# Attention probabilities of the last two query tiles turned by VectorE blocks and a trip through DRAM, with their value products put off

## The chip, the cores and the metric

The kernel runs on one core of a Trainium2 chip. The metric is the time of one execution on the device in microseconds (us). Five engines work side by side in that core: TensorE (PE in the rows; PEld is its loading of weights), VectorE (DVE), ScalarE (ACT), GpSimd (POOL) and SyncE (SP), which issues all of this kernel's transfers. The core has an on-chip memory of 128 partitions (SBUF) and the accumulation banks that TensorE writes (PSUM).

## The reference, cut to what matters

The model is a trunk of two layers over 1024 positions of width 1024. Each layer runs a convolution branch and a sparse attention branch from one input projection and joins them in one output projection. The change lies in the attention branch:

```python
def block_fn(args):                      # one block of 128 queries (blk = 0..7)
    ...
    score = jnp.einsum("bth,bths->bts", w_b, jax.nn.relu(s_raw))
    _, sel = lax.top_k(score, k_top)     # 256 keys for each query
    ...
    logits = logits + bias.astype(jnp.float32)
    probs = jax.nn.softmax(jnp.where(valid, logits, -jnp.inf), axis=-1)
    return jnp.einsum("bthk,btkc->bthc", probs.astype(kv.dtype), kv_sel)
...
y = jnp.concatenate([y_conv, y_attn], axis=-1) @ w_out[l]
```

There are 8 heads. The kernel doesn't gather: it computes the logits against all earlier keys and pushes the unselected ones out with a large constant, so query tile i (128 queries, i = 0 to 7) has 128 * (i + 1) keys.

## The kernel before, in words

**Order of a layer.** Projections, indexer and convolution run first, then `topk` picks keys, then `attention` (line 801), then `Split` (line 912) cuts the two branch outputs into a high and a low float32r part, then `out_proj` (line 933) multiplies them by the output weights in four column groups g = 0 to 3, and the next layer follows. Layer 0's attention lies at about 355 to 545 us of the profile, layer 1's at about 985 to 1147 us.

**Attention.** The heads are taken in pairs, pr = 0 to 3, and within a pair the query tiles in couples c: tiles 2c and 2c+1. The order of c is 0, 1, 2, 3 in the first three pairs and `LASTC` = 3, 1, 2, 0 in the last. For each couple, for each of the two heads e and the two tiles ii:
- `probs` (line 818) multiplies queries by keys into PSUM (tile `lg`, three float32r products a piece, lines 112 to 114), adds bias and mask (GpSimd line 837 or 834), takes the row minimum on VectorE (lines 843 and 847), the exponential on ScalarE (line 850), the reciprocal (line 851), and scales on GpSimd (line 852). The result `p` has queries on partitions.
- `transposed` (line 859) turns `p` by TensorE, 128x128 at a time (line 865), into PSUM (tag `tp`, two banks), and copies it to tiles `pt` in turn by ScalarE (line 870) and VectorE (line 872), so that keys lie on partitions.

Then the value products of the couple (line 893) run into one PSUM bank (`av`, tag `mm`), alternating between the two heads, and VectorE multiplies by the gate (line 896). Each of these matmuls stands as two records in the profile.

**Queries.** `queries(h)` (line 803) makes the high and low query tile of one head, in two halves of 512 columns through a PSUM bank of tag `mm` (`uq`), and loads the head's bias (`tb`). The next pair's two heads are called for after the second and the third couple of a pair.

**Buffers.** Every tag has a fixed number of buffers, and a tile whose tag has none free waits until one is released after its last reader. Those that matter: `hp`, 6 buffers of 4 KB a partition: four for the two heads in work (high and low each), two left; the high halves `yh` of `Split` use the same tag (four for the convolution branch `yc`, two for the attention branch `ya`, which shares its tile with `An` and stands so in the rows). `hq`, 6, for `pt`. `hv`, 4, for the values `v`, and later two of the `yh`. `t4`, 5, for `p`. PSUM `mm`, 2 banks, shared by `av`, `uq` and half of the output tiles `o`; `lg`, 4 banks. `pl`, 1, used by `topk` and then by the second half of the output weights of group 0.

**Who orders the work.** In attention no order is written out by hand: a list scheduler places each instruction on its engine's in-order queue, earlier lines of the program first where several are ready, at the times of its own timing model. `tc.issue_after(x)` only orders an instruction behind x on x's engine. All transfers go out by SyncE's in-order queue.

**Around the end of attention.** In the last pair, parts of `Split(yc)` are called for after each couple; `Split(ya)` follows attention. In `out_proj`, group 0 takes the query tiles in the order 6, 7, 2, 3, 4, 5, 0, 1, and each output tile sums eight k: 0 to 3 from `yc`, 4 to 7 from `ya`.

Of the kernel before, what the change touches and what calls it, by code (L numbers as in the profile page):

```python
# [11 lines left out]
F32 = mybir.dt.float32  # L12
# [11 lines left out]
P = 128  # L24
# [52 lines left out]
def hybrid_kernel(ctx: ExitStack, tc: tile.TileContext, x, cT, w_ada, w_mod, bcol, bgate, g_pre, w_in, w_cp,  # L77
# [20 lines left out]
    def st(tag, shape, dt=F32, name=None, bufs=None):  # L98
        return sb.tile(shape, dt, name=name or tag, tag=tag, bufs=bufs or BUFS.get(tag, 1))
# [701 lines left out]
    def attention(l, cq, kv, v, sc, sga, wq, select, yc):  # L801

        def queries(h):
            qt = [st("hp", [P, 1024], FR, name="q%d" % i) for i in range(2)]
            for half in range(2):
                hs = slice(512 * half, 512 * half + 512)
                o = mm_ps("uq")
                for k in range(2):
                    mm3(o, tuple(x_[:, 128 * h:128 * h + 128] for x_ in wq[k]),
                        (cq[:, k, hs], cq[:, 2 + k, hs]), k == 0, k == 1)  # L810
                S.activation(qt[0][:, hs], o, AF.Copy, scale=-QSCALE)
                V.scalar_tensor_tensor(qt[1][:, hs], o, -QSCALE, f32(qt[0][:, hs]), op0=OP.mult,
                                       op1=OP.subtract)
            tb = st("t5", [P, 256], name="tb")
            nc.sync.dma_start(tb, td[h])
            return qt, tb

        def probs(q, tb_, i):

            w = P * (i + 1)  # L820
            o = []
            for c0, c1 in pieces(i):
                o.append((lg_ps("lg"), c0, c1))
                mm3(o[-1][0][:, :c1 - c0], tuple(x_[:, 128 * i:128 * i + 128] for x_ in q),
                    tuple(x_[:, c0:c1] for x_ in kv), True, True)
            n0 = max(0, w - 256)
            nw = w - n0
            tb = tb_[:, 256 - nw:]
            p = st("t4", [P, 1024], name="p")
            nb = p[:, n0:w]  # L830
            if i < 2:
                if nw > 128:
                    V.tensor_copy(nb[:, 0:nw - 128], tb[:, 0:nw - 128])
                G.affine_select(nb[:, nw - 128:nw], tb[:, nw - 128:nw], pattern=[[-1, P]],
                                compare_op=OP.is_ge, fill=BIG, base=0, channel_multiplier=1)
            else:
                G.tensor_tensor(nb, tb, sc[:, OFF[i] + n0:OFF[i] + w], op=OP.add)  # L837
            m = st("mx", [P, 3], name="mx", bufs=8)
            lo = FMAX
            for o_, c0, c1 in o:  # L840
                if c0 < n0:
                    e = min(c1, n0)
                    V.tensor_tensor_reduce(out=p[:, c0:e], in0=o_[:, :e - c0], in1=sc[:, OFF[i] + c0:OFF[i] + e],
                                           scale=1.0, scalar=lo, op0=OP.add, op1=OP.min,
                                           accum_out=m[:, c0 // 384:c0 // 384 + 1])
                    lo = m[:, c0 // 384:c0 // 384 + 1]
            V.tensor_tensor_reduce(out=nb, in0=o_[:, n0 - c0:w - c0], in1=nb, scale=1.0, scalar=lo,  # L847
                                   op0=OP.add, op1=OP.min, accum_out=m[:, 2:3])
            ri = st("ri", [P, 2], name="ri", bufs=8)
            mark[0] = S.activation(p[:, :w], p[:, :w], AF.Exp, scale=-1.0, bias=m[:, 2:3], accum_out=ri[:, 0:1])  # L850
            V.reciprocal(ri[:, 1:2], ri[:, 0:1])  # L851
            mark[1] = G.tensor_scalar(p[:, :w], p[:, :w], ri[:, 1:2], 1.0, op0=OP.mult, op1=OP.mult)  # L852
            return p

        turn = [0]
        late = [[], []]
        mark = [None, None]

        def transposed(p, i, ii, pts):

            for j0 in range(0, i + 1, 4):
                n = min(4, i + 1 - j0)
                t = tp_ps("pt")
                for j in range(n):
                    T.transpose(t[:, 128 * j:128 * j + 128], p[:, 128 * (j0 + j):128 * (j0 + j) + 128], ident)  # L865
                dst = pts[j0 // 4][:, 0:n, 128 * ii:128 * ii + 128]
                src = t[:, :128 * n].rearrange("p (j t) -> p j t", j=n)
                turn[0] += 1
                if turn[0] % 2:
                    late[1].append(S.activation(dst, src, AF.Copy).ins)  # L870
                else:
                    late[0].append(V.tensor_copy(dst, src).ins)  # L872

        nxt = [queries(0), queries(1)]
        for pr in range(4):
            cur = nxt
            nxt = []
            if pr == 1:
                dump(f"sel{l}", sc)
            for at, c in enumerate((0, 1, 2, 3) if pr < 3 else LASTC):  # L880
                pts = [[st("hq", [P, 4, 256], name="pt") for _ in range(1 + c // 2)] for e in range(2)]
                for e in range(2):
                    for ii in range(2):
                        i = 2 * c + ii
                        p = probs(*cur[e], i)
                        transposed(p, i, ii, pts[e])
                o = mm_ps("av")
                for j in range(2 * c + 2):
                    for e in range(2):
                        h = 2 * pr + e  # L890
                        lh = v[j // 2][:, j % 2, 64 * h:64 * h + 64]
                        t0 = 128 if j == 2 * c + 1 else 0
                        T.matmul(o[64 * e:64 * e + 64, t0:256], lh, pts[e][j // 4][:, j % 4, t0:256],  # L893
                                 start=j == 0, stop=j == 2 * c + 1)
                g = sga[:, pr, 256 * c:256 * c + 256]
                V.tensor_tensor(g, o[:, :256], g, op=OP.mult)
                if (pr, c) == (2, 2):
                    with tc.issue_after(mark[0].ins), tc.issue_after(mark[1].ins):
                        w0 = wo_load(l, 0, 0)
                if at in (1, 2) and pr < 3:  # L900
                    nxt.append(queries(2 * pr + 2 + (at == 2)))
                if pr == 0 and at < 2:
                    select(4 + at)
                elif pr == 3 and at < 3:
                    with tc.issue_after(late[0][-1]), tc.issue_after(late[1][-1]):
                        if at == 0:
                            ys = Split(yc, ["hp"] * 4)
                        for n in range(3 * at, min(3 * at + 3, 8)):
                            ys.part(n // 2, 512 * (n % 2), 512, V)
        return w0, ys  # L910
# [332 lines left out]
```

## Time and profile before

| | us |
|---|---|
| median of 3 runs | 1235.65 (1235.15 to 1236.28) |
| the profiled execution, its own time | 1234.0 |
| the profiled execution, span of the trace | 1232.2 |
| TensorE busy in the span | 1173.8 (95%) |
| VectorE, ScalarE, GpSimd busy | 897.0, 701.9, 606.5 |

The time of an execution holds 1.8 us around its span. Busy shares are averages over stages that have different limits; what a change in one stage is worth is read from the rows of that stage.

### The profile page before, as it was taken

To read this page: it belongs to the slowest core of one execution; us is meant where nothing else is said; L and a number is where in the kernel's file an instruction comes from. 1 tells how busy PE (TensorE), PEld (TensorE's weight loads), DVE (VectorE), ACT (ScalarE), POOL (GpSimd) and SP (SyncE) were. 2 spreads that over 40 slices of the span, in tenths; PEclk is the share of its full clock that TensorE was granted. 3 is DMA by queue.
4 is the path that set the end of the run, shared out by engine and by line. 5 is a ranking of instruction groups with operands and counts; after the bars stand their busy time and mean duration, and the time that the engine had idled before them with its cause. 6 is when DMAs were issued, how large, how long until landed. Compare 5 with 4: busy or idle time off the path is not lost.

```text
span 1232.2 us, 23069 instructions
## 1 busy us (share of the span) xinstructions
PE 1173.8 (95%) x7832; PEld 975.8 (79%) x7832; DVE 897.0 (73%) x2182; ACT 701.9 (57%) x1616; POOL 606.5 (49%) x1218
## 2 busy tenths in 40 slices
PE   6999999999987999999999999999999599999998
PEld 3788888877875777789989888888798377777998
DVE  4657788898798656757686688898888876667214
ACT  4545767766864556643254376785687355566221
POOL 4431136547548548635483211553864665685222
PEclk9999999999998999999999999999999699999999
DMA  9520258852100001148651122894111000021205
GB/s 352 201 85 18 69 195 274 275 171 75 35 27 1 9 10 47 33 127 292 235 196 34 46 52 74 270 289 160 58 30 43 1 10 5 6 77 63 76 18 189
DMA packets 93158, 130.20 MB, mean 106 GB/s; under 512 B 41576, under 2 KB 70768, under 8 KB 93040
## 3 DMA queue, kind: packets, MB, share of 16 engines
q1 hardware_dynamic: 93040, 128.73, 32.5%
q8 instruction: 62, 1.02, 0.3%
q14 instruction: 56, 0.46, 0.1%
HBM read 115.06 MB, written 13.64 MB: 104 GB/s over the span
## 4 chain that ended last, share of the span: by engine, by line
PE 85%; DVE 5%; POOL 5%; issue 2%; ACT 1%; DMA 1%; SPq 0%; DVEq 0%; POOLq 0%; ACTq 0%
PE av L893 7%; PE pt L865 5%; PE ixs L476 5%; PE u L112 5%; PE u L113 5%; PE u L114 5%; PE g L112 5%; PE g L114 4%; PE g L113 4%; PE o L112 4%; PE o L113 4%; PE o L114 4%; PE lg L112 3%; PE cv L674 2%; PE lg L113 2%; PE lg L114 2%
## 5 line engine op out<-in xcount | busy, mean ns | idle before, releaser
L559 DVE TENSOR_SCALAR_CACHE_REDUCE jv<-pl,cand 128x768 int8<-128x768 uint16 (+1 forms) x186 | 187.9, 1010 | 30.8 <-POOL cand L566 20.0
L554 ACT ACTIVATE ja<-pl,cand 128x896 int8<-128x896 uint16 (+1 forms) x186 | 154.1, 829 | 60.6 <-POOL cand L566 45.7
L850 ACT ACTIVATE p<-p,mx 128x128 f32<-128x128 f32 (+7 forms) x128 | 98.7, 771 | 57.1 <-DVE mx L847 49.1
L852 POOL TENSOR_SCALAR p<-p,ri 128x128 f32<-128x128 f32 (+7 forms) x128 | 99.6, 784 | 39.6 <-DVE ri L851 39.2
L133 POOL TENSOR_TENSOR wul<-raw,wuh 128x342 fp32r<-128x342 f32 (+1 forms) x48 | 46.9, 1000 | 129.3 <-ACT wuh L132 123.3
L112 PE MATMUL o<-woh,yh 128*128 128x256 f32 x384 | 109.5, 286 | 0.0
L114 PE MATMUL o<-woh,yl 128*128 128x256 f32 x384 | 108.6, 283 | 0.0
L113 PE MATMUL o<-wol,yh 128*128 128x256 f32 x384 | 108.1, 282 | 0.0
L865 PE MATMUL pt<-ident,p 128*128 128x128 f32 x576 | 94.4, 282 | 10.2 <-POOL p L852 7.7
L112 PE MATMUL u<-hT,wuh 128*128 128x512 f32 x256 | 101.4, 396 | 0.0
L112 PE MATMUL g<-hT,wgh 128*128 128x512 f32 x256 | 101.2, 395 | 0.0
L114 PE MATMUL u<-hT,wul 128*128 128x512 f32 x256 | 100.0, 391 | 0.0
L113 PE MATMUL u<-hT,wuh 128*128 128x512 f32 x256 | 99.9, 390 | 0.0
L113 PE MATMUL g<-hT,wgh 128*128 128x512 f32 x256 | 99.8, 390 | 0.0
L114 PE MATMUL g<-hT,wgl 128*128 128x512 f32 x256 | 99.7, 389 | 0.0
L837 POOL TENSOR_TENSOR p<-tb,score 128x256 f32<-128x256 f32 x96 | 75.5, 793 | 47.4 <-PE pt L865 47.3
L893 PE MATMUL av<-pt,v 128*64 128x256 f32 (+1 forms) x640 | 94.9, 372 | 1.9 <-DVE pt L872 1.8
L112 PE MATMUL lg<-kvT,q 128*128 128x384 f32 (+2 forms) x192 | 78.5, 410 | 18.3 <-DVE mx L847 18.2
L865 PEld LDWEIGHTS pt<-ident,p 128*128 128x128 f32 x576 | 67.8, 142 | 33.6 <-issue 13.6
L490 DVE SCALAR_TENSOR_TENSOR score<-relu,widx,score 128x384 f32<-128x384 f32 (+2 forms) x84 | 78.8, 976 | 18.8 <-ACT relu L482 18.1
L482 ACT ACTIVATE relu<-ixs 128x512 f32<-128x512 f32 (+2 forms) x140 | 66.7, 523 | 35.8 <-PE ixs L476 35.4
L966 ACT ACTIVATE ja<-o 128x256 int8<-128x256 f32 x64 | 24.5, 383 | 107.2 <-PE o L114 107.0
(294 smaller groups left out, 3439.7 us busy)
## 6 DMA issues: line engine op xcount, KB each, us to landing
wt<-in_wl_dram SPq DMA_DIRECT2D x64, 512.0 KB, 5.7
wa<-in_w_mod_dram SPq DMA_DIRECT2D x32, 512.0 KB, 4.9
raw<-in_w_in_dram SPq DMA_DIRECT2D x64, 171.0 KB, 2.7
wa<-in_w_ada_dram SPq DMA_DIRECT2D x16, 512.0 KB, 10.1
raw<-in_w_out_dram SPq DMA_DIRECT2D x32, 171.0 KB, 2.7
raw<-in_w_in_dram SPq DMA_DIRECT2D x32, 170.0 KB, 2.7
ad<-A SPq DMA_DIRECT2D x8, 512.0 KB, 3.7
at<-ad SPq DMA_DIRECT2D x16, 256.0 KB, 5.1
```

The lines of the kernel that those rows point to most:

```text
L112: T.matmul(o, ah, bh, start=first, stop=False)
L113: T.matmul(o, ah, bl, start=False, stop=False)
L114: return T.matmul(o, al, bh, start=False, stop=last)
L482: S.activation(r[:, c0:c1], o[:, :c1 - c0], AF.Relu)
L490: V.scalar_tensor_tensor(acc, r[:, :w], wc, acc, op0=OP.mult, op1=OP.add)
L554: S.activation(ja[:, :wid(j)], src, AF.Sign, scale=-1.0, bias=col(cand, c), accum_out=col(ct_, c))
L559: V.tensor_scalar(jv[:, :wid(j)], src, col(cand, c), None, op0=OP.is_lt, op1=OP.add, accum_out=col(ct_, c))
L837: G.tensor_tensor(nb, tb, sc[:, OFF[i] + n0:OFF[i] + w], op=OP.add)
L850: mark[0] = S.activation(p[:, :w], p[:, :w], AF.Exp, scale=-1.0, bias=m[:, 2:3], accum_out=ri[:, 0:1])
L852: mark[1] = G.tensor_scalar(p[:, :w], p[:, :w], ri[:, 1:2], 1.0, op0=OP.mult, op1=OP.mult)
L865: T.transpose(t[:, 128 * j:128 * j + 128], p[:, 128 * (j0 + j):128 * (j0 + j) + 128], ident)
L893: T.matmul(o[64 * e:64 * e + 64, t0:256], lh, pts[e][j // 4][:, j % 4, t0:256], start=j == 0, stop=j == 2 * c + 1)
```

## The change

For the couple c = 3 (tiles 6 and 7) `transposed` is replaced by `turned`. VectorE transposes the 32x32 blocks of `p` in place of the whole, in two instructions a tile (512 columns, then 384 or 512), into a staging tile `stage` of tag `pl`. Four transfers of 128 KB a tile, one for each band of 32 partitions, write it to a DRAM tile `pd` (4 buffers) in runs of 512 bytes, and two transfers of 256 KB read it back in runs of 2 KB with keys on partitions, into tiles of tag `hp` (four tiles for a couple: two heads, two halves of the keys). A tile's read is queued behind the next tile's writes. The value products of that couple are no longer called for at once: they come after the second couple of the next pair (in the last pair: those of pair 2 after the first couple, those of pair 3 after the third), queued behind the last logit product called for until then. `mark` gets a third place to hold that product. The numbers of buffers are unchanged.

```diff
--- before.py
+++ after.py
@@ -821,8 +821,8 @@
             o = []
             for c0, c1 in pieces(i):
                 o.append((lg_ps("lg"), c0, c1))
-                mm3(o[-1][0][:, :c1 - c0], tuple(x_[:, 128 * i:128 * i + 128] for x_ in q),
-                    tuple(x_[:, c0:c1] for x_ in kv), True, True)
+                mark[2] = mm3(o[-1][0][:, :c1 - c0], tuple(x_[:, 128 * i:128 * i + 128] for x_ in q),
+                              tuple(x_[:, c0:c1] for x_ in kv), True, True)
             n0 = max(0, w - 256)
             nw = w - n0
             tb = tb_[:, 256 - nw:]
@@ -854,7 +854,7 @@
 
         turn = [0]
         late = [[], []]
-        mark = [None, None]
+        mark = [None, None, None]
 
         def transposed(p, i, ii, pts):
 
@@ -871,29 +871,82 @@
                 else:
                     late[0].append(V.tensor_copy(dst, src).ins)
 
+        stage = st("pl", [P, 2, 2, 4, 4, 32], name="stage")
+        V.memset(stage[:, 0, 1, :, 3, :], 0.0)
+
+        back = []
+
+        def turned(p, ii, pts):
+
+
+            s = stage[:, ii]
+            for h, n in ((0, 4), (1, 3 + ii)):
+                V.transpose(s[:, h, :, 0:n, :],
+                            p[:, 512 * h:512 * h + 128 * n].rearrange("p (j q t) -> p q j t", q=4, t=32))
+            d = dr.tile([2, 4, 32, 4, 128], F32, name="pd", tag="pd", bufs=4)
+            for a in range(4):
+                w = nc.sync.dma_start(d[:, :, :, a, :].rearrange("h q s c -> s (h q) c"),
+                                      s[32 * a:32 * a + 32].rearrange("s h q j t -> s (h q) (j t)"))
+            if back:
+                with tc.issue_after(w.ins):
+                    back.pop()()
+
+            def read():
+                for h in range(2):
+                    nc.sync.dma_start(pts[h][:, ii].rearrange("p a j t -> p (a j t)"),
+                                      d[h].rearrange("q s a c -> (q s) (a c)"))
+
+            back.append(read)
+
+        def values(pr, c, pts, after=None):
+
+            o = mm_ps("av")
+            with nullcontext() if after is None else tc.issue_after(after.ins):
+                products(o, pr, c, pts)
+            g = sga[:, pr, 256 * c:256 * c + 256]
+            V.tensor_tensor(g, o[:, :256], g, op=OP.mult)
+
+        def products(o, pr, c, pts):
+            for j in range(2 * c + 2):
+                for e in range(2):
+                    h = 2 * pr + e
+                    lh = v[j // 2][:, j % 2, 64 * h:64 * h + 64]
+                    ii = j == 2 * c + 1
+                    pt = pts[e][j // 4]
+                    T.matmul(o[64 * e:64 * e + 64, 128 * ii:256], lh,
+                             pt[:, ii:2, :, j % 4, :] if c == 3 else pt[:, j % 4, 128 * ii:256],
+                             start=j == 0, stop=j == 2 * c + 1)
+
         nxt = [queries(0), queries(1)]
+        open_ = []
         for pr in range(4):
             cur = nxt
             nxt = []
             if pr == 1:
                 dump(f"sel{l}", sc)
             for at, c in enumerate((0, 1, 2, 3) if pr < 3 else LASTC):
-                pts = [[st("hq", [P, 4, 256], name="pt") for _ in range(1 + c // 2)] for e in range(2)]
+                if c == 3:
+                    pts = [[st("hp", [P, 2, 4, 4, 32], name="pd") for _ in range(2)] for e in range(2)]
+                else:
+                    pts = [[st("hq", [P, 4, 256], name="pt") for _ in range(1 + c // 2)] for e in range(2)]
                 for e in range(2):
                     for ii in range(2):
                         i = 2 * c + ii
                         p = probs(*cur[e], i)
-                        transposed(p, i, ii, pts[e])
-                o = mm_ps("av")
-                for j in range(2 * c + 2):
-                    for e in range(2):
-                        h = 2 * pr + e
-                        lh = v[j // 2][:, j % 2, 64 * h:64 * h + 64]
-                        t0 = 128 if j == 2 * c + 1 else 0
-                        T.matmul(o[64 * e:64 * e + 64, t0:256], lh, pts[e][j // 4][:, j % 4, t0:256],
-                                 start=j == 0, stop=j == 2 * c + 1)
-                g = sga[:, pr, 256 * c:256 * c + 256]
-                V.tensor_tensor(g, o[:, :256], g, op=OP.mult)
+                        if c == 3:
+                            turned(p, ii, pts[e])
+                        else:
+                            transposed(p, i, ii, pts[e])
+                if back:
+                    back.pop()()
+                for w in open_:
+                    w[0] += c + 1
+                if open_ and open_[0][0] >= 3:
+                    values(*open_.pop(0)[1], mark[2])
+                if c == 3:
+                    open_.append([0, (pr, c, pts)])
+                else:
+                    values(pr, c, pts)
                 if (pr, c) == (2, 2):
                     with tc.issue_after(mark[0].ins), tc.issue_after(mark[1].ins):
                         w0 = wo_load(l, 0, 0)
```

## Rows read from the trace of the kernel before

**Rows 1.** The page: the span; busy time, share and instructions of each engine.

```profile
span 1232.2 us, 23069 instructions
...
PE 1173.8 (95%) x7832; PEld 975.8 (79%) x7832; DVE 897.0 (73%) x2182; ACT 701.9 (57%) x1616; POOL 606.5 (49%) x1218
```

**Rows 2.** Busy time by stretch, layer 0; behind POOL: granted clock, DMA share, GB/s.

```profile
412.60:452.30 39.70, 39.65 (x250) 29.43 (x251) 25.94 (x103) 21.61 (x48) 21.55 (x32) 1.00 0.03 8
452.30:492.80 40.50, 40.26 (x245) 29.16 (x245) 27.66 (x107) 25.12 (x56) 28.95 (x40) 1.00 0.12 36
...
360.00:380.00 20.00, 10.19 (x36) 7.19 (x34) 18.27 (x38) 8.37 (x18) 15.53 (x15) 0.74 0.00 1
485.70:522.40 36.70, 36.18 (x247) 27.14 (x246) 26.89 (x96) 24.32 (x52) 26.68 (x33) 1.00 0.12 35
522.40:555.60 33.20, 33.19 (x271) 29.47 (x270) 19.02 (x45) 15.34 (x45) 12.24 (x20) 1.00 0.39 123
```

**Rows 3.** The chain of waits, 452 to 494 us: shares by line; start, us, what.

```profile
by line: PE av L893 27.1%; PE pt L865 21.5%; PE lg L112 12.8%; PE lg L113 11.6%; PE lg L114 11.1%; PE uq L112 5.9%; PE uq L114 4.4%; PE uq L113 4.4%; ACT pt L870 1.4%; issue 0.4%
...
457.63 0.87 PE pt L865 x8
...
459.43 1.88 PE av L893 x16
```

**Rows 4.** Who waited for whom, 412 to 540 us: total, times, longest.

```profile
POOL p L837 <- PE pt L865: 20.6, 21, 2.7
```

**Rows 5.** VectorE's groups by shape, 452.3 to 492.8 us (pair 2).

```profile
L872 DVE COPY pt<-pt 128x512 f32<-128x512 f32 x4 | 2.7, 687 | 0.7 <-PE pt L865 0.5
...
L872 DVE COPY pt<-pt 128x384 f32<-128x384 f32 x2 | 1.1, 553 | 0.6 <-PE pt L865 0.6
```

**Rows 6.** VectorE's groups by shape, 355 to 400 us.

```profile
L613 DVE TENSOR_TENSOR_SCAN score<-eq 128x512 f32<-128x512 f32 x1 | 1.2, 1219 | 0.0
...
L612 DVE TENSOR_SCALAR eq<-score,tf 128x512 f32<-128x512 f32 x1 | 0.5, 483 | 0.0
```

**Rows 7.** TensorE's groups by shape, whole span.

```profile
L674 PE MATMUL cv<-wt,at 128*32 128x128 f32 x1024 | 31.3, 274 | 0.0
L893 PE MATMUL av<-pt,v 128*64 128x128 f32 x128 | 26.2, 288 | 0.0
```

**Rows 8.** SyncE's queue in order of time, 480 to 545 us.

```profile
486.38 0.33 SPq L815 DMA_DIRECT2D tb<-td  x1
```

**Rows 9.** DMA issues: count, KB each, median us from issue to landing.

```profile
ad<-A SPq DMA_DIRECT2D x8, 512.0 KB, 3.7
...
out_dram<-xr SPq DMA_DIRECT2D x16, 256.0 KB, 3.2
...
tb<-td SPq DMA_DIRECT2D x16, 128.0 KB, 2.0
```

**Rows 10.** ScalarE in order of time, 510 to 534 us.

```profile
512.97 1.66 ACT L923 ACTIVATE yh<-yc 128x512 fp32r<-128x512 f32 x3
...
522.65 1.14 ACT L923 ACTIVATE yh<-yc 128x512 fp32r<-128x512 f32 x2
```

**Rows 11.** TensorE in order of time, 520 to 527 us.

```profile
522.13 0.28 PE L114 MATMUL lg<-kvT,q 128*128 128x256 f32 x1
...
525.25 0.28 PE L112 MATMUL o<-woh,yh 128*128 128x256 f32 x1
```

**Rows 12.** TensorE in order of time, 429.5 to 439 us: start, us, instruction.

```profile
430.35 0.65 PE L893 MATMUL av<-pt,v 128*64 128x256 f32 x2
430.93 0.50 PE L112 MATMUL uq<-cq,wuqh 128*128 128x512 f32 x1
...
436.37 1.73 PE L893 MATMUL av<-pt,v 128*64 128x256 f32 x14
```

**Rows 13.** TensorE, 485 to 486.3 us: pair 3's first logits (head 6, tile 6).

```profile
485.72 0.39 PE L112 MATMUL lg<-kvT,q 128*128 128x512 f32 x1
```

**Rows 14.** ScalarE, 520 to 560 us: the eighth output tile of group 0.

```profile
555.64 0.38 ACT L966 ACTIVATE ja<-o 128x256 int8<-128x256 f32 x1 [0.31 <-PE o L114]
```

## The prediction

> **What bounds the kernel now.** I read the page first: TensorE is busy for 95% of the span, VectorE for 73% [rows 1]. A share over the whole span says nothing of one stage, so I cut layer 0's attention into pairs of heads. In pairs 1 and 2 TensorE is busy for 39.65 of 39.70 us and 40.26 of 40.50 us at the full granted clock, VectorE for 26 to 28 us, ScalarE and GpSimd for less than 29 us [rows 2]. The chain of waits says the same: in the 42 us from 452 to 494 it runs over TensorE almost without a break, 21.5% of it on the transposes (line 865) and 27.1% on the value products [rows 3]. Even GpSimd's wait to start a new `p` is mostly a wait for those transposes, because they release the buffers of `p`: 20.6 us in 128 us [rows 4]. So in this stage a TensorE instruction that goes away is worth its time, as long as nothing else takes its place.
>
> **What is removed.** Tiles 6 and 7 have 7 + 8 blocks a head, 30 transposes a pair, 120 a layer, 240 in all. Price: 21.5% of 42 us is 9.0 us for a pair's 72 transposes, 0.125 us each; the run of eight gives 0.87 / 8 = 0.109 [rows 3]. So 3.3 to 3.8 us a pair, 26 to 30 us in all. Eight PSUM copies a pair go too, half on ScalarE, half on VectorE: two of 0.687 and two of 0.553 us there, 2.5 us [rows 5].
>
> **What is added on VectorE.** Eight block transposes a pair, six of 512 columns and two of 384. No row shows one. Below, the cheapest 512-column operation from SBUF takes 0.483 us; above, the scan takes 1.219 us [rows 6]. I take the copies' 0.687 and 0.553, since both pass 512 elements a lane once: 5.2 us a pair (bounds 3.7 to 9.2). VectorE then has 27.7 - 2.5 + 5.2 = 30.4 us in a pair [rows 2]. The most that VectorE reached in a stretch that it bounds is 18.27 of 20 us, 0.91 [rows 2], so it needs 33.4 us a pair, still less than TensorE's 40.1 - 3.8 = 36.3.
>
> **The value products' new operand** is read in runs of 32 elements. The convolution's products read theirs so too: 274 ns for 128 columns, against 288 ns for a value product of 128 columns in one run [rows 7]. Cost: nothing.
>
> **Transfers.** A tile costs four writes of 128 KB and two reads of 256 KB. SyncE needs about 0.33 us to issue one [rows 8], so 24 a pair are 8 us of a queue that has little else to do; what queues behind them there is the bias `tb` and the output weights. Landing: 2.0 us for 128 KB, 3.2 for 256 KB, 3.7 for 512 KB [rows 9]. One tile's trip is about 1.4 + 2.5 + 0.7 + 3.2 = 8 us. The value products were put off by two couples, about 12 us of TensorE's work, and that would cover it.
>
> **What the cover overlooks: `hp`.** The new `pd` tiles need four `hp` buffers a pair, and `hp` has six: four hold the current queries, two the next head's. That this tag is short is seen at the end of attention: `yh<-yc` gets two buffers at 512.97, and the third only at 522.65, just after head 6's last logits at 522.13 [rows 10, 11]. Tags are also served in program order: `uq` runs 0.58 us after the first `av` product, although the rest of that group comes only at 436.37 [rows 12]: it had to let `av` take its bank first. So pair 0's first two `pd` get the buffers of head 1's queries, but the last two wait until head 2 has made its last logits, late in pair 1. Its value products, called for after two couples, run only then and hold one of the two `mm` banks until then; the next queries wait behind them. I count from head 2's last logits: 1.4 us issue and 3.2 to 3.7 landing, 5 us; value products 2 x 1.88 = 3.8 us [rows 3], to 9 us; the next pair's queries by 7 to 12 us. VectorE still has two heads' tiles 6 and 7 to finish in that time, 10 us or more, so the pairs keep flowing, but less evenly. Of the 3.8 us a pair I take 2 in pairs 1 and 2 (between none and all) and 1 in pair 0, whose first part VectorE bounds. That is 5 us a layer.
>
> **The end of attention.** Pair 3 begins at 485.72 [rows 13], head 6's last logits are at 522.13 [rows 11], and group 0's eighth output tile is done at 555.64 [rows 14]: 36.4 + 33.5 = 69.9 us, TensorE never idle [rows 2], because output products fill it from 525.25 [rows 11]. After the change: in the first part TensorE loses 3.8 us of transposes, and 12 us of value products that can't run yet, so VectorE sets the pace. It has 26.9 us there now [rows 2]; minus four `Split` parts (2.6) and the copies (2.5), and plus 5.2, less one gate product, it is 26.6, at 0.91: 29.2 us. Then, from head 6's last logits: 5 us to read pair 2's last `pd`, 3.8 us of value products (9); head 7's writes, which had waited for DRAM buffers, 5 us beside that (10); its reads 4 us (14); pair 3's value products 3.8 us (18). Only now are buffers free for the other `yh`, so 14 parts of `Split` follow, ten of 0.57 us (half of 1.14 [rows 10]) and four shorter, 7 us (25), while TensorE starts on group 0: 8 tiles x 24 products x 0.117 us = 22.5 us, of which 3.5 are done by then. The remaining 19 start at 20 and end, with 2 us of waits, at 41. Sum 29.2 + 41 = 70.2, 0.3 more than now.
>
> **Sum.** (5 - 0.3) x 2 layers = 9.4 us. From the execution's own 1234.0 us this gives 1224.6; the median of the runs stands 1.65 higher, so I predict 1226.
>
> **Rivals.**
> - *A: the end of attention doesn't shrink first.* If pair 3 keeps its 36.4 us (its tiles 6 and 7 come first, with the heads' queries just made) and the `Split` parts run before most output products instead of beside them (25.5 + 19 = 44.5), the end takes 80.9 in place of 69.9. With the 5 us from the pairs, a layer loses 6: 1235.65 + 12 = 1248. It decides from the point where pair 3 and group 0 together take more than 75 us. For it: six buffers, and a chain of two DRAM trips in series. Against it: TensorE's work in pair 3 falls from 36 to some 22 us.
> - *B: VectorE's transposes are dear.* At the scan's 1.219 us they cost 9.2 us a pair; a pair then needs (27.7 - 2.5 + 9.2) / 0.91 = 37.8 us of VectorE, just under what I took, but pair 3's first part 33.6: a layer gains 5 - 4.7 = 0.3, no change, 1235. For it: the unknown price. Against it: nothing in such a block move is a dependent scan. The Trainium skill, "VectorE: DVE Perf Modes", section "The three transpose paths", puts 128x128 at 311 ns on VectorE and 390 ns on TensorE, and advises TensorE for a whole 128x128 transpose, since VectorE turns only 32x32 blocks; that is a rule against this change. By its figure (bf16) a 512-column instruction would take an estimated 1.24 us, case B, while a TensorE transpose costs only 0.109 to 0.125 us in the chain here [rows 3], far below its 390 ns.
> - *C: the buffers don't bind* (slots given to whoever is ready): TensorE stays the limit everywhere and the whole 26 to 30 us come back: 1208.
>
> **How the numbers follow.** Chances: forecast 0.45, A 0.30, B 0.15, C 0.10. The forecast's own range is 1217 to 1234 (pairs giving 1 to 3.3 us each, the end 3 us better or worse). The range for 8 in 10 leaves out most of C and the upper part of A: 1210 to 1249. Less than 0.2% (2.5 us) is about what a measurement here can't tell from no change. Faster: nearly all of the forecast and C, 0.53; same: most of B and edges of the others, 0.14; slower: A and the rest, 0.33.
>
> **What the profile after would show.** Right: 336 transposes at line 865 in place of 576, VectorE transposes near 0.69 us; pairs near 38 us; reads into `pd` of the second head only after the next pair's first head has made its last logits; `yh<-yc` not before the end of attention; from pair 3's first logits to group 0's eighth tile about 70 us. Wrong: `pd` reads right behind their writes (C), or a stretch of over 75 us at the end with TensorE idle for more than 10 (A), VectorE at 0.9 all through (B). A drop of the granted clock in the last pair, where TensorE is less busy than now, would cost on top of A.

## The result, and the profile after

The changed kernel takes 1227.97 us (median of 6 runs, 1224.72 to 1230.37); the kernel before takes 1235.70 (1234.33 to 1236.28, 6 runs). The ratio is 0.9936, 95% interval [0.9916, 0.9957]: 7.7 us faster. The prediction was 1226, in the range 1210 to 1249, with 0.53 on faster. The profiled execution of after is the slowest of its six, 1230.37 us; what follows compares it with the profiled execution of before at 1234.0, and so shows 3.6 us where the medians show 7.7. Two runs of e3 and one of e7 fell into a slower state and are left out of the medians below.

The page of after: span, then busy time, share and instructions of each engine.

```profile
span 1228.6 us, 22954 instructions
...
PE 1153.0 (94%) x7592; PEld 957.0 (78%) x7592; DVE 917.2 (75%) x2216; ACT 683.4 (56%) x1584; POOL 605.1 (49%) x1218
```

Against [rows 1] TensorE has 240 instructions and 20.8 us of busy time less, VectorE 20.2 us more. The span fell by 3.6 us only. So most of what left TensorE did not leave the time, and the question of the experiments is where it stayed.

The groups of after by line for the transposes that stayed on TensorE, and by shape for those on VectorE (count | busy us, mean ns | idle before them):

```profile
L865 PE MATMUL pt<-ident,p 128*128 128x128 f32 x336 | 59.8, 292 | 13.5 <-POOL p L852 11.3 <-ACT pt L870 2.0
...
L884 DVE STREAM_TRANSPOSE stage<-p 128x512 f32<-128x512 f32 x48 | 32.4, 695 | 2.2 <-issue 1.3 <-DMA pd<-stage 0.6
...
L884 DVE STREAM_TRANSPOSE stage<-p 128x384 f32<-128x384 f32 x16 | 8.6, 535 | 0.0
```

336 transposes are left of 576. VectorE's take 0.695 and 0.535 us, where the copies whose price was borrowed took 0.687 and 0.553 [rows 5]. The Trainium skill, "VectorE: DVE Perf Modes", section "The three transpose paths", gives 311 ns for 128x128 in bf16, which would have made it an estimated 1.24 us for 512 columns. This trace does not agree: a 128x512 float32 instruction takes little more than half of that.

The transfers of after (count, KB each, median us from issue to landing):

```profile
pd<-stage SPq DMA_DIRECT2D x128, 128.0 KB, 2.5
pd<-pd SPq DMA_DIRECT2D x64, 256.0 KB, 4.1
```

Writes land in the 2.5 us assumed, reads in 4.1 in place of 3.2 [rows 9].

To see where the time went, I cut each kernel's attention at the first logits of each pair and at the end of the evacuation of group 0's eighth output tile (both read from the order in time of TensorE and ScalarE). Layer 1's first logits stand at 950.1 us in before, not at the 985 us named further up. In us, layer 0 / layer 1:

| kernel | pair 0 | pair 1 | pair 2 | pair 3 and group 0 | sum |
|---|---|---|---|---|---|
| before | 50.3 / 58.3 | 39.6 / 39.6 | 40.1 / 40.0 | 70.3 / 70.3 | 200.2 / 208.2 |
| after | 51.4 / 58.0 | 33.7 / 34.3 | 41.6 / 41.6 | 72.8 / 70.0 | 199.5 / 204.0 |

Before rounding, the first three pairs gain 3.2 and 3.9 us a layer, the end loses 2.5 and gains 0.3. That is 4.9 us in all; 1.3 us of it is lost outside attention. That the gain stands in pair 1 alone comes from the cut: late work of pair 1 falls into pair 2, which in layer 0 holds 98 records of value products and 30 of query products, against 78 and 12 in pair 1 (80 and 24 in either pair before). The busy time of these stretches in after, layer 0 (pairs 1, 2, 3, and group 0; behind POOL: granted clock, DMA share, GB/s):

```profile
407.10:440.80 33.70, 32.27 (x207) 24.23 (x205) 28.62 (x113) 18.58 (x44) 22.61 (x35) 1.00 0.57 158
440.80:482.40 41.60, 40.45 (x249) 29.19 (x249) 29.64 (x112) 22.04 (x51) 26.22 (x38) 1.00 0.50 130
482.40:512.50 30.10, 25.65 (x130) 18.92 (x130) 23.76 (x87) 15.22 (x33) 19.30 (x26) 0.94 0.64 159
512.50:555.20 42.70, 40.05 (x315) 34.10 (x314) 22.30 (x50) 19.87 (x55) 16.23 (x26) 0.96 0.61 201
```

Pair 1 has 207 TensorE instructions and pair 2 has 249; in the last two rows TensorE is idle for 7.1 us and its granted clock is below 1, where before it was idle for 0.5 us in the same part and at 1.00 [rows 2].

What TensorE waits for there: pair 3 of after, in order of time on TensorE (start, us, what, and in brackets the idle time before it and what ended it).

```profile
495.19 0.41 PE L112 MATMUL lg<-kvT,q 128*128 128x384 f32 x1 [0.59 <-DVE mx L847]
...
497.34 0.47 PE L112 MATMUL lg<-kvT,q 128*128 128x512 f32 x1 [1.39 <-DVE mx L847]
...
500.90 0.55 PE L865 MATMUL pt<-ident,p 128*128 128x128 f32 x3 [0.90 <-POOL p L852]
502.26 0.66 PE L865 MATMUL pt<-ident,p 128*128 128x128 f32 x4 [0.81 <-POOL p L852]
...
509.17 0.29 PE L114 MATMUL lg<-kvT,q 128*128 128x256 f32 x1
...
516.52 5.11 PE L916 MATMUL av<-pd,v 128*64 128x256 f32 x30 [2.09 <-DMA pd<-pd]
...
529.55 3.45 PE L916 MATMUL av<-pd,v 128*64 128x256 f32 x30
```

First it waits for VectorE (which has to release a logits bank) and for GpSimd behind it, then for a read from DRAM. The row at 509.17 is head 6's last logits; the two rows behind it are the put-off value products of pair 2 and of pair 3. The `Split` parts came late, as forecast: the first from `yc` (ScalarE in order of time) start at 521.47, where before three had started at 512.97 [rows 10].

```profile
521.47 2.19 ACT L976 ACTIVATE yh<-yc 128x512 fp32r<-128x512 f32 x4 [2.56 <-PE av L916]
...
531.11 2.19 ACT L976 ACTIVATE yh<-yc 128x512 fp32r<-128x512 f32 x4 [1.66 <-PE av L916]
...
554.83 0.38 ACT L1019 ACTIVATE ja<-o 128x256 int8<-128x256 f32 x1 [0.31 <-PE o L114]
```

The last of these rows is the eighth output tile, 0.8 us earlier than before [rows 14].

Next, after in order of time, late in pair 1: the last logits of head 2 (TensorE, first two rows), then SyncE's reads into the second head's `pd`, and TensorE's value products of pair 0 (`av<-pd`), with the queries of pair 2 on either side of them.

```profile
431.26 0.40 PE L113 MATMUL lg<-kvT,q 128*128 128x512 f32 x1
431.49 0.40 PE L114 MATMUL lg<-kvT,q 128*128 128x512 f32 x1
...
431.73 1.78 SPq L896 DMA_DIRECT2D pd<-pd  x4
...
433.38 0.39 PE L112 MATMUL uq<-cq,wuqh 128*128 128x512 f32 x1
...
437.33 3.43 PE L916 MATMUL av<-pd,v 128*64 128x256 f32 x30 [0.36 <-DMA pd<-pd]
...
441.62 0.39 PE L112 MATMUL uq<-cq,wuqh 128*128 128x512 f32 x1
```

This is the chain that the prediction forecast: the reads issue as soon as head 2's queries are free, the value products follow at 437.33, and the second half of the next queries comes behind them at 441.62. That it happens is shown. What it costs, and whether the buffers are to blame, is not yet.

### The profile page after: what moved, and what is told of

The parts are those of the page before. It is cut to its first block, busy times and chain, and to the rows that moved or that the text cites. A ratio compares the mean times of both kernels' runs of the same rounds, so it can differ in the third digit from the quotient of the medians.

```text
span 1228.6 us, 22954 instructions
## 1 busy us (share of the span) xinstructions
PE 1153.0 (94%) x7592; PEld 957.0 (78%) x7592; DVE 917.2 (75%) x2216; ACT 683.4 (56%) x1584; POOL 605.1 (49%) x1218
## 5 line engine op out<-in xcount | busy, mean ns | idle before, releaser
L476 PE MATMUL ixs<-ix 128*128 128x512 f32 (+2 forms) x320 | 76.3, 356 | 0.5 <-ACT relu L482 0.5
L112 PEld LDWEIGHTS o<-woh,yh 128*128 128x128 f32 x384 | 73.3, 191 | 1.4 <-ACT yh L976 0.8
L113 PEld LDWEIGHTS o<-wol,yh 128*128 128x128 f32 x384 | 73.3, 191 | 0.0
```

The costliest lines, as they stand in the source:

```text
L112: T.matmul(o, ah, bh, start=first, stop=False)
L113: T.matmul(o, ah, bl, start=False, stop=False)
L476: mark = T.matmul(o[:, :c1 - c0], s_[:, 128 * i:128 * i + 128], ix[:, kk, c0:c1], start=kk == 0, stop=kk == 1)
```

## The experiments

Theory of the prediction: what the transposes free on TensorE is lost because six `hp` buffers are too few. Its rivals after the result: the DRAM trip itself; VectorE's extra work; the order in which TensorE meets the value products. Each ratio is against runs of the kernel before on the same chip, with its 95% interval.

**e1: buffers of their own for the second head.**

```diff
-    pts = [[st("hp", [P, 2, 4, 4, 32], name="pd") for _ in range(2)] for e in range(2)]
+    pts = [[st(("hp", "w4")[e], [P, 2, 4, 4, 32], name="pd") for _ in range(2)] for e in range(2)]
```

> The second head's `pd` tiles come from the tag `w4` instead of `hp`, so that they need not wait for the next pair's queries to go; the first head's stay in `hp`. Theory 1 (the six `hp` buffers are what keeps the change from its 26 to 30 us): the reads of the second head's `pd` follow their writes at once, the value products run before the next pair's last logits, the last pair is shorter by the wait of about 8 us, and the pairs come nearer to 36.3 us: 1212 to 1218 us. Theory 2 (VectorE paces the changed pairs, buffers or not): the reads come earlier, but the pairs keep their 38 us and the time stays at 1225 to 1231 us.

Measured: 1234.45 us, ratio 0.9982 [0.9969, 0.9994]. Neither: slower than the changed kernel by 6.5 us. In the profiled executions that loss stands in layer 1 alone: its attention, cut as in the table above, takes 209.9 us against after's 204.0, layer 0's takes 198.0 against 199.5. TensorE's waits in layer 1's attention, e1 (us in total, times, longest):

```profile
PE av L916 <- DMA pd<-pd: 8.1, 3, 3.6
PE av L916 <- issue: 1.4, 1, 1.4
```

With the buffers free, the value products move forward to the place that the program gives them, two couples behind, and there TensorE stands until the reads land (6.7 us of such waits in layer 0). Pairs 1 and 2 become even (37.2 and 37.9 us in layer 0), but are not shorter than after's mean of 37.7.

**e2: the new way in pairs 0 and 1 alone** (`new` replaces `c == 3` in the three places that choose).

```diff
+                new = c == 3 and pr < 2
-                if c == 3:
+                if new:
```

> Only pairs 0 and 1 of a layer use the new way; tiles 6 and 7 of pairs 2 and 3 are transposed on TensorE and their values are made at once. Theory 1 (the end of attention neither gains nor loses; a pair in the middle gains 2 us): about half the pairs' gain is left, 1229 (1227 to 1232) us. Theory 2 (the last pair loses several us a layer to the wait for buffers, TensorE idle and its clock halved there): without this loss the kernel is faster than the changed one, 1220 to 1224 us.

Measured: 1226.30 us, ratio 0.9925 [0.9906, 0.9943]. Between the two; its interval covers the changed kernel's ratio. So pairs 2 and 3 of each layer, half of the change, bring nothing that can be measured: the gain is made by pairs 0 and 1, and what the last pairs save on TensorE is lost at the end of attention. In after, pair 3 and group 0 have 443 TensorE instructions in place of 519, and take 72.8 and 70.0 us in place of 70.3.

**e3: every block transpose twice.**

```diff
-                V.transpose(s[:, h, :, 0:n, :],
...
+                for _ in range(2):
+                    V.transpose(s[:, h, :, 0:n, :],
...
```

> Each block transpose on VectorE is done twice, the same result written again: 64 more instructions of 0.53 to 0.69 us, 41 us of VectorE in all, 5.2 us a pair. Theory 1 (TensorE or the buffers set the pace and VectorE has slack): most of it is hidden, 1228 to 1240 us. Theory 2 (VectorE sets the pace in the changed pairs): most of the 41 us shows, 1255 to 1270 us.

Measured: 1248.8 us, ratio 1.0101 [1.0079, 1.0123], 21 us more than the changed kernel, between both ranges. The expected 41 us are a sum of durations, and on VectorE an instruction's record overlaps the next one's. The page of e3 shows what was really added: 948.4 - 917.2 = 31.2 us of busy time.

```profile
PE 1157.6 (93%) x7592; PEld 956.8 (77%) x7592; DVE 948.4 (76%) x2280; ACT 683.1 (55%) x1584; POOL 603.8 (48%) x1218
```

So about two thirds of VectorE's extra work show and one third is hidden; the transposes' own time can't be taken as free either.

**e4: putting off without turning.** Transposes on TensorE and copies as before, into the new layout, with the second head's `pd` in `w4`.

```diff
+                if put_off:
+                    dst = pts[j0 // 4][:, ii, :, 0:n, :].rearrange("p a j t -> p j a t")
+                    src = t[:, :128 * n].rearrange("p (j a t) -> p j a t", j=n, a=4)
...
-                        if c == 3:
-                            turned(p, ii, pts[e])
-                        else:
-                            transposed(p, i, ii, pts[e])
+                        transposed(p, i, ii, pts[e], c == 3)
```

> Tiles 6 and 7 are transposed on TensorE and copied out of PSUM as in the kernel before, into `pd` tiles of the new layout (the second head's in the tag `w4`, as in e1); the value products are put off as in the changed kernel. There is no VectorE transpose and no DRAM trip. Theory 1 (the gain comes from the transposes that leave TensorE; putting off is only the price of the DRAM trip): the time of the kernel before, 1235 (1231 to 1240) us, and e1 is faster than it by 15 us or more. Theory 2 (part of the gain comes from the order, since TensorE no longer stands at value products that wait for late copies): 1225 to 1231 us.

Measured: 1231.18 us, ratio 0.9960 [0.9946, 0.9974], on the border of both ranges. But the interval leaves no change out: putting off (with the buffers of e1) gains some 4.6 us, with all 576 transposes still on TensorE and no DRAM trip, and e1 is not faster than it, as theory 1 wanted, but slower. That is theory 2's kind. Pair 2, first before and then e4, same columns as above:

```profile
445.70:485.70 40.00, 39.76 (x249) 29.20 (x248) 25.78 (x103) 23.48 (x54) 26.18 (x39) 1.00 0.12 33
```

```profile
445.60:483.90 38.30, 37.97 (x249) 29.65 (x248) 25.74 (x101) 23.78 (x55) 25.66 (x38) 1.00 0.09 27
```

The same 249 instructions, 99% busy in both, and 1.7 us less. 1.4 us of that is in the value products: counted up to the next start, their 80 records take 10.97 us in before and 9.58 in e4. The theory put this down to waits for late copies; the traces show something else. In order of time on TensorE, three runs of value products and what follows each, first before (two runs), then e4:

```profile
447.26 1.95 PE L893 MATMUL av<-pt,v 128*64 128x256 f32 x16
449.13 0.66 PE L865 MATMUL pt<-ident,p 128*128 128x128 f32 x4
...
455.24 0.65 PE L893 MATMUL av<-pt,v 128*64 128x256 f32 x2
455.82 0.50 PE L112 MATMUL lg<-kvT,q 128*128 128x512 f32 x1
```

```profile
460.44 0.43 PE L920 MATMUL av<-pt,v 128*64 128x256 f32 x1
...
464.54 0.39 PE L112 MATMUL lg<-kvT,q 128*128 128x256 f32 x1
```

A run of 16 records takes 1.87 us, 0.117 us each; a run of 2 takes 0.58 us, 0.29 each; e4's run of 40 (16 of them of 128 columns) takes 4.10 us, 0.103 each. Every run of two in this stretch takes 0.57 to 0.58 us in both kernels, whatever ran before it, which a wait for a copy would not do. Before cuts the pair's 80 records into ten runs, e4 into six: (10.97 - 9.58) / 4 is 0.35 us for each run less. So what e4 gains here is fewer changes from one kind of product to another. That this price of a run holds in the other kernels too is not shown.

**e5: no trip.** No writes, no reads, no `pd` buffers.

```diff
-            d = dr.tile([2, 4, 32, 4, 128], F32, name="pd", tag="pd", bufs=4)
...
-                    pts = [[st("hp", [P, 2, 4, 4, 32], name="pd") for _ in range(2)] for e in range(2)]
+                    pts = [[v[2 * e + h].rearrange("p a (b j t) -> p a b j t", b=4, j=4) for h in range(2)]
+                           for e in range(2)]
```

> VectorE turns tiles 6 and 7 as in the changed kernel, but nothing is written to DRAM or read back: their value products read a constant tile (the values themselves, in the same strides) in place of the probabilities, and no `pd` tiles are held. Left out: the way of the probabilities to their partitions. Theory 1 (the trip through DRAM and the buffers it holds eat the gain): TensorE sets the pace again and 15 us or more come back, 1205 to 1213 us. Theory 2 (what VectorE has to do more, and what waits for it, eats the gain): at most 6 us faster than the changed kernel, 1220 to 1228 us.

Measured: 1214.15 us, ratio 0.9828 [0.9815, 0.9841], just outside theory 1's range and far from theory 2's. The trip and all that hangs on it (buffers, order, DMA, and the waits of value products for their probabilities, which e5's don't have) cost the changed kernel 13.8 us. VectorE does as much as in after, so it is not what holds after at 1228; but it is near. Pair 3 of e5:

```profile
477.20:510.00 32.80, 29.53 (x192) 21.72 (x192) 28.30 (x101) 20.77 (x46) 22.50 (x29) 1.00 0.07 20
```

VectorE is busy for 28.30 of 32.80 us there, and TensorE is idle for 3.3.

**e6: e1, put off by three couples.**

```diff
-                if open_ and open_[0][0] >= 3:
+                if open_ and open_[0][0] >= 6:
```

> As e1 (the second head's `pd` in `w4`), but the value products are put off by three couples in place of two. Theory 1 (e1 lost because its value products stand at the head of TensorE's fixed order and wait there for the reads from DRAM, 8.1 us in layer 1's attention): these waits go, 1219 to 1226 us. Theory 2 (VectorE's pace, not the reads, holds e1 back): 1231 to 1236 us, as e1.

Measured: 1229.31 us, ratio 0.9949 [0.9937, 0.9961], 5.1 us better than e1, between the two ranges. The pairs are shorter than in e1 (36.7 and 36.7 us in layer 0), but the end takes 72.8 and 75.0 us.

**e7: e2 with the value products of pairs 2 and 3 put off too** (their `pd` tiles in `hp` and `w4`, as in e4).

```diff
-                        if c == 3:
+                        if c == 3 and pr < 2:
                             turned(p, ii, pts[e])
                         else:
-                            transposed(p, i, ii, pts[e])
+                            transposed(p, i, ii, pts[e], c == 3)
```

> Pairs 0 and 1 as in the changed kernel; tiles 6 and 7 of pairs 2 and 3 are transposed on TensorE, as in e2, but their value products are put off, as in e4. Theory 1 (putting off is worth 1.2 to 1.4 us a pair by itself, the wait of value products for the PSUM copies): four pairs more than e2, 1219 to 1223 us. Theory 2 (what e4 gained is already in e2, or `w4` costs what the order gives): 1225 to 1228 us, as e2.

Measured: 1225.9 us, ratio 0.9923 [0.9908, 0.9938]: theory 2, as e2. What the order gives in e4 is not added to what the turning gives in e2, or the buffers that it takes cost as much.

**e8: value products at once.**

```diff
-                if c == 3:
-                    open_.append([0, (pr, c, pts)])
-                else:
-                    values(pr, c, pts)
+                values(pr, c, pts)
```

> As the changed kernel, but the value products of tiles 6 and 7 come right behind their couple, as in the kernel before. Theory 1 (TensorE's order is fixed, so it stands at these products for the DRAM trip of about 8 us): 4 to 8 us more for each of 8 pairs, 1260 to 1290 us. Theory 2 (enough other work stands ahead of them in the order to cover the trip): 1226 to 1236 us.

Measured: 1230.55 us, ratio 0.9955 [0.9939, 0.9972]: theory 2, 2.6 us behind the changed kernel. The program's call is hardly what puts these products off. In e8 the reads for pair 0's second head issue at 434.1 and its value products run at 439.5; in after, 431.7 and 437.3. The `hp` buffers set the place in both.

**e9 and e10: no `pd` in `hp` at all, two couples and three.** The tag becomes `("hq", "w4")[e]`; e10 adds the edit of e6.

> All `pd` tiles leave `hp`: the first head's come from `hq`, the second head's from `w4`; put off by two couples, as in the changed kernel. Theory 1 (the 14 us between the changed kernel and e5 are the buffers: in e1 the first head's `pd` still took two `hp` buffers from the next queries): 1214 to 1221 us. Theory 2 (they are the trip itself: with the buffers free the value products come to stand in TensorE's order before their reads have landed): 1226 to 1234 us, with TensorE waiting for the reads as in e1.

> As e9, but put off by three couples in place of two. Theory 1 (buffers): as e9 in the first three pairs, and up to 6 us a layer later at the end of attention, where the last value products then come after the last logits, as in e6: 1217 to 1228 us. Theory 2 (trip): 3 us a layer better than e9 in pairs 0 to 2, the same loss at the end: 1225 to 1232 us.

Measured: e9 1233.88 us, ratio 0.9995 [0.9979, 1.001]; e10 1221.79 us, ratio 0.9891 [0.9879, 0.9904]. e9 is theory 2's, e1 over again. e10 lies in theory 1's range, with its reason refuted by e9, and below theory 2's: one couple more is worth 12 us.

**e11: the changed kernel, put off by three couples.** The edit of e6 alone.

> The changed kernel with its `pd` tiles in `hp`, put off by three couples in place of two: the fourth corner beside the changed kernel (`hp`, two), e9 (`hq` and `w4`, two) and e10 (`hq` and `w4`, three). Theory 1 (both were needed: the buffers of `hp` bind as long as `pd` and the queries share them): 1225 to 1232 us, no better than the changed kernel. Theory 2 (only the number of couples mattered in e10): 1219 to 1224 us.

Measured: 1219.18 us, ratio 0.9874 [0.9854, 0.9894]: theory 2. It is the fastest of the kernels that do the whole computation, with e10 behind it (their runs overlap), and 8.8 us faster than the changed kernel and 15.8 faster than before, by one number. Its stretches, layer 0 (pairs 1, 2, 3, and group 0):

```profile
406.30:437.70 31.40, 29.94 (x180) 22.59 (x178) 25.72 (x103) 16.40 (x41) 21.16 (x33) 1.00 0.52 144
437.70:474.20 36.50, 35.54 (x224) 26.49 (x222) 27.62 (x108) 21.00 (x50) 23.95 (x36) 1.00 0.51 141
474.20:505.80 31.60, 27.99 (x160) 20.27 (x160) 27.53 (x96) 15.04 (x31) 19.25 (x25) 0.95 0.68 166
505.80:548.10 42.30, 41.18 (x334) 35.19 (x335) 23.41 (x54) 22.56 (x63) 19.96 (x32) 1.00 0.62 217
```

Pairs 1 and 2 take 67.9 us in place of 75.3, with 52 TensorE instructions fewer; pair 3 and group 0 take 49 more of them in 73.9 us in place of 72.8. The work moved into the stretch where TensorE was idle. At e4's 0.12 us a record (an estimate; 50 of the 52 are records of value products) the 52 are 6.2 of the 7.4 us that pairs 1 and 2 are shorter. That leaves about 1 us for the pairs themselves and about 5 for the end, which does 6 us more work in 1.1 us more. In layer 1 the same count gives 3 us for the pairs and 1.4 for the end. Late in pair 1 of e11, in order of time (SyncE's reads, TensorE's queries and value products):

```profile
425.17 0.50 PE L112 MATMUL uq<-cq,wuqh 128*128 128x512 f32 x1
...
434.02 0.48 PE L112 MATMUL uq<-cq,wuqh 128*128 128x512 f32 x1
...
439.35 2.80 PE L916 MATMUL av<-pd,v 128*64 128x256 f32 x22
```

```profile
432.45 1.78 SPq L896 DMA_DIRECT2D pd<-pd  x4
```

The reads issue as late as in after (432.45 against 431.73). But both halves of the queries now stand ahead of the value products, 8 us earlier than in after (425.17 and 434.02 against 433.38 and 441.62), and no TensorE wait for reads of more than 0.6 us in all is left in layer 0.

**e12: e10 with every block transpose twice** (the edit of e3).

> e10 with each block transpose done twice, 41 us more of VectorE. Theory 1 (with buffers and trip out of the way TensorE sets the pace and VectorE has some 5 us of slack a pair): less than half of it shows, 1222 to 1240 us. Theory 2 (VectorE now sets the pace, as the last pair of e5 with 19.08 of 20 us suggests): 1250 to 1263 us.

Measured: 1250.67 us, ratio 1.0131 [1.0108, 1.0154], at the low edge of theory 2. VectorE is busy for 951.4 us here and for 917.7 in e10: 28.9 of these 33.7 us show. Some of it is clock, lost while TensorE waits: the mean granted clock is 0.970 here and 0.983 in e10, at most 16 us of the span. With the transposes doubled the better order is worth nothing (e3: 1248.8). So VectorE has little slack left once the order is mended.

The placing as a grid, medians in us:

| `pd` buffers | at once | two couples | three couples |
|---|---|---|---|
| `hp` | 1230.55 (e8) | 1227.97 (after) | 1219.18 (e11) |
| `hp`, `w4` | | 1234.45 (e1) | 1229.31 (e6) |
| `hq`, `w4` | | 1233.88 (e9) | 1221.79 (e10) |

Along a row, the third couple is worth 5 to 12 us. Down a column, no kernel with freed buffers is faster than the one with all `pd` in `hp`. But that is not the same as buffers that cost nothing: e10 differs from e6 only in the first head's `pd`, which leave `hp`, and is 7.5 us faster. In layer 0 both have 215 and 220 TensorE instructions in pairs 1 and 2, in 73.4 us (e6) and 73.3 (e10), and 468 and 467 in pair 3 and group 0. There e6 takes 72.8 us and e10 69.2 (layer 1: 75.0 and 70.7). The first `Split` parts of `yc`, which need `hp`, show it, first e6, then e10:

```profile
511.41 2.17 ACT L976 ACTIVATE yh<-yc 128x512 fp32r<-128x512 f32 x4
```

```profile
485.59 1.66 ACT L976 ACTIVATE yh<-yc 128x512 fp32r<-128x512 f32 x3
```

So at three couples the shortage of `hp` costs about 4 us a layer, all of it at the end of attention. At two couples nothing of this shows: with e9's freed buffers the end takes 73.4 and 74.4 us.

## Why the prediction was right, and where it was not

- **The time.** 9.4 us were forecast, 7.7 measured. The terms are not as near as the sum: in the profiled execution attention gains 4.9 us, and the reasons behind the terms are half right. So the closeness is in part luck.
- **The price on VectorE** was right: 0.695 and 0.535 us. That closes rival B as it was put, a dear transpose. **The strided operand** costs nothing: the median record of a value product is 379 ns from `pd` and 379 from `pt`.
- **The pairs.** 5 us a layer were forecast, 3.2 and 3.9 measured. **The end of attention**: 70.2 us forecast from pair 3's first logits to the start of the eighth evacuation, 72.4 and 69.6 measured (69.9 before). Two misses partly cancel in it. Up to head 6's last logits 29.2 us were forecast and 26.8 and 26.6 measured, with VectorE busy for 23.76 of 30.10 us in layer 0, 0.79 and not 0.91. From there 41 us were forecast and 45.7 and 43.0 measured: in layer 0 pair 3's put-off value products start 20.4 us after those logits, where 14 were forecast. Rival A's turning point of 75 us was not reached, but the idle TensorE that it spoke of came (7.1 us), and the halved clock with it. e2 agrees: the last two pairs give nothing.
- **The step that failed in kind is "What the cover overlooks: `hp`".** Its facts are right: late reads, the held bank, the queries behind it. Its inference, that the shortage of buffers is what keeps 26 to 30 us down to 10, is refuted for the pairs: freed buffers make the kernel slower at two couples (e1, e9), and the fastest kernel reads just as late (e11). At the end of attention the shortage does cost something, about 4 us a layer at three couples (e6 against e10). What counts at least as much is where the value products are called for. Two couples lose with `hp` (the queries stand behind the value products) and without it (TensorE waits for the reads). The "12 us of TensorE's work" that were to cover an 8 us trip did not cover it: e1 shows 6.7 and 8.1 us of waits in the two layers.
- **A gain that the sum did not have.** Putting off was costed as cover only. e4 shows that it is worth 4.6 us by itself. The reading that failed is that a TensorE busy for 39.65 of 39.70 us has nothing to give but instructions that go away: the same instructions took some 1.7 us a pair less in longer runs.
- **Where the rest of 26 to 30 us went.** e5 puts 13.8 us on the trip and what hangs on it, and e11 wins 8.8 back by one couple more. Beyond that VectorE is near: once the order is mended, 28.9 of 33.7 us more of its work show, the clock that TensorE loses meanwhile included (e12). Rival C's 1208 was reached by no kernel.
- **Left open.** Why freed buffers cost 6 us at two couples: the waits for reads are only a part (e9 has 3.1 and 2.9 us of them), e1 loses in layer 1 alone, and whether the tags that gave the buffers (`w4`, `hq`) then ran short was not tried. How much of e11's gain is the earlier queries, how much the filled idle time, and how much the clock (mean granted 0.981 in e11, 0.974 in after) is not separated; the estimate above puts the first two differently in each layer. Three couples in pairs 0 to 2 with two in pair 3, whose end takes 75.0 us in e11's layer 1, was not tried.

## What to carry to other kernels

When results take a detour (DRAM, another engine), where their consumer stands in a fixed order can be worth more than half of the detour (8.8 of 13.8 us here): try the consumer one step later before adding buffers, and look at what is called for behind it (here the next queries). Then ask for each stage by itself whether buffers are short. An engine at 99% busy can still have time to give: compare start-to-start times of the same instructions between two orders, and count the runs that they are cut into. A cost moved to an engine with slack on average shows as soon as the order is mended, so double it once to learn how much slack there is, and take what was added from the engine's busy time.

## What the hardware showed

A float32 block transpose of 128x512 on VectorE takes 0.695 us, about as long as a plain copy out of PSUM (0.687 us). Value products cost more the shorter the run in which TensorE meets them: 0.29 us a record in a run of 2, 0.117 in a run of 16 (before, layer 0's pair 2).

TensorE's granted clock was at the lower of its two levels (1.2 GHz) for two stretches of 3.4 us in the last pair of after's layer 0, from 503.4 and 517.1 us, each behind idle time of TensorE (1.39, 0.90 and 0.81 us before the first; 2.09 us before the second). The second fell on value products: 30 records took 5.11 us, in pair 1 at the full clock 3.43. In before, with TensorE idle for 0.5 us there, the clock stayed at 1.00 [rows 2]. Idle time alone did not always bring the drop: e5's pair 3 has 3.3 us of it at 1.00. So work taken off TensorE just where it then idles can give part of its gain back in clock.
